# Mixers paced to slot 97, one route moved to the next phase, an eleventh row buffer and a 4 KB descriptor ring

## The chip, the cores and the metric

One core of one Trainium2 chip runs the whole kernel in one launch. The metric is the device time of that launch in microseconds. The kernel before takes 1519.63 us (median of three runs, 1519.27 to 1521.75).

## What is computed

A decoder trunk of two layers over one sequence of 256 tokens with 1024 channels, in float32. The reference, cut to what matters:

```python
for l in range(DEPTH):                       # 2 layers
    proj = x @ w_in[l]                       # 1024 -> 2464 columns, split over four mixers
    mix = concat([short_conv, mla_attention, conformer_conv, swa_sink_attention])
    mix = rms_norm_per_head(mix) * gain
    h = layer_norm(ALPHA * x + mix @ w_out[l])
    x = layer_norm(ALPHA * h + peer_ffn(h))

def peer_ffn(h):                             # per chunk of 128 tokens
    q = (h @ w_q).reshape(c, 8, 2, 128)      # 8 heads, two halves
    sc = einsum('chpd,hpnd->chpn', q, sub_keys)
    # top 16 of 128 in each half, then top 16 of the 256 sums: 16 expert numbers per head
    gate = softmax(best_s)
    act = gelu(einsum('chkd,cd->chk', u_tab[idx], h))
    return einsum('chk,chkd->cd', gate * act, v_tab[idx])
```

Each token picks 8 heads x 16 experts = 128 experts out of 16384, and each expert is one row of u and one row of v (1024 floats each). The rows of 256 tokens x 128 experts x 2 layers are most of what the kernel reads.

## The kernel before

**Tiles and phases.** The 256 tokens are two tiles of 128 (t = 0, 1). For each layer l and tile t there is a *phase* of 128 *slots*; in slot k every token of the tile gets its k-th expert. The four phases run one after another: (0,0), (0,1), (1,0), (1,1), here called phases 0 to 3. Ahead of them lie the mixer of (0,0) and the route of its first head.

**A slot** (`peer`, line 738): GpSimd (POOL) issues an indirect DMA that gathers one row per token, u and v side by side, 128 partitions x 8 KB, into a buffer `row` (line 760). VectorE (DVE) multiplies the u half with h and sums it (the *product*, line 763). For the slot before, `post` then runs GELU and the gate on ScalarE (ACT, lines 745, 746), makes a diagonal of the result (line 748), and TensorE (PE) multiplies that diagonal with the v half into the two PSUM accumulators (line 750), which the profile shows as four passes of 128x512.

**Row buffers.** `row` comes from the pool `gp` with `ROWS` = 10 buffers. A gather can be issued when a buffer's last matmul is done. The tiles for `w_out` of the later mixers (line 579, tag `row`) and, at the start, the pieces of `w_in` of the first layer take buffers of the same pool.

**Other work beside the slots.** A phase's slots leave room on PE, DVE and ACT, and other tasks are woven in:
- `route(l, t, hd)` (line 661) computes one head's expert numbers and gates: 32 passes for the queries (line 680), 4 for the scores (line 685), then the two rounds of top 16 on DVE (lines 655 to 659). A head must be routed before the slots that use it. The weights of a head are 1152 KB. Tile 0 uses the heads in the order 0 to 7, tile 1 in the order 5, 6, 7, 0, 1, 2, 3, 4 (`HEADS`).
- `mix(l, t)` (line 289) is a mixer with its projections, attention and convolutions, the output projection (line 585) and a layer norm. It loads nine pieces of `w_in` and four of `w_out`. The mixer of tile 1 must end before any head of tile 1 is routed.
- `finish` is the layer norm that ends a phase; it runs in slots 0 to 3 of the next.

**Weight buffers.** `load_w` (line 162) uses a pool of three buffers for pieces of `w_in` and heads' weights, issued on SyncE's queue (SP). Heads 0, 1, 2 have buffers of their own (`HELD`). Heads 5, 6, 7 (`KEPT`) are the *joint* heads: their weights are loaded for tile 0 and kept in the three buffers until tile 1 has been routed with them, so they load once.

**The order of the work** is written out in `main_loop` (line 852): a list of tasks with a first slot, a last slot and a cost (`MIX` = 111, `ROUTE` = 10.9, `TAIL` = 6.6). `paced` (line 805) steps through the slots and advances each task in proportion, so a mixer given slots 0 to 80 is spread evenly over them. `keep_behind` lets the engines' order stray from this by six slots. Before, tile 0's phase has heads 2 to 6 in slots 0 to 80 beside the mixer of tile 1, and then four routes in 48 slots: joint heads 5, 6 and 7 of tile 1 and head 7 of tile 0, two of them at once between slots 80 and 97.

Of the kernel before, what the change touches and what calls it, by code (L numbers as in the profile page):

```python
# [33 lines left out]
QK = KC * 256 + 256  # L34
PPC = 8 + 6 + 62 + 2

ROWS = 10

HELD = (0, 1, 2)
KEPT = (5, 6, 7)  # L40
# [20 lines left out]
MIX, ROUTE, TAIL = 111.0, 10.9, 6.6  # L61
# [3 lines left out]
def kernel(ctx: ExitStack, tc: tile.TileContext, x, positions, w_in, w_att, bcast, perch, lnrows, lncols,  # L65
                      w_out, w_qk, uv, ident, mla_mask, swa_dist, iota, invf, out):
    nc = tc.nc
# [6 lines left out]
    sp = ctx.enter_context(tc.tile_pool(name="sp", bufs=2))  # L74
    gp = ctx.enter_context(tc.tile_pool(name="gp", bufs=ROWS))
    pm = ctx.enter_context(tc.tile_pool(name="pm", bufs=4, space=bass.MemoryType.PSUM))
# [661 lines left out]
    def peer(l, t, h, acc):  # L738

        n = NH * TOPK  # L740
        order = HEADS[t]
        prev = None

        def post(k, act, row, gate):
            S.activation(act, act, AF.Gelu)  # L745
            S.activation(act, act, AF.Copy, scale=gate[:, k % TOPK:k % TOPK + 1])  # L746
            dg = gp.tile([P, P], F32, tag="dg", name="dg", bufs=3)
            S.activation(dg, idn, AF.Copy, scale=act)  # L748
            for j in range(2):
                nc.tensor.matmul(acc[j], dg, row[:, DM + j * 512:DM + (j + 1) * 512],  # L750
                                 start=(k == 0), stop=(k == n - 1))

        for k in range(n):
            while (l, t, order[k // TOPK]) not in R:
                yield None
            ix8, ix, gate = R[l, t, order[k // TOPK]]
            if ix8 is not None and k % TOPK < 8:
                ix = ix8
            row = gp.tile([P, 2 * DM], F32, tag="row", name="row")
            nc.gpsimd.indirect_dma_start(out=row, out_offset=None, in_=uv,  # L760
                                         in_offset=bass.IndirectOffsetOnAxis(ap=ix[:, k % TOPK:k % TOPK + 1], axis=0))
            act = gp.tile([P, 1], F32, tag="act", name="act", bufs=3)
            V.scalar_tensor_tensor(row[:, :DM], row[:, :DM], 1.0, h, op0=ALU.mult, op1=ALU.mult, accum_out=act)  # L763
            if prev is not None:
                post(*prev)
            prev = (k, act, row, gate)
            yield 1
        post(*prev)

    def finish(l, t, h, acc):  # L770
        hp = mp.tile([P, DM], F32, tag="S", name="hp2")
        for j in range(2):
            sl = slice(j * 512, (j + 1) * 512)
            V.scalar_tensor_tensor(hp[:, sl], h[:, sl], ALPHA, acc[j], op0=ALU.mult, op1=ALU.add)
        yield 1.2
        xo = xp.tile([P, DM], F32, tag="x", name=f"x{t}_{l}")
        yield from layer_norm(xo, hp, 4 * l + 2, out[t * P:(t + 1) * P, :] if l == L - 1 else None)
        X[t] = xo
# [5 lines left out]
    def mix(l, t):  # L784
        if t == 0:
            Y[l] = layer_state(l)
        H[l, t] = yield from mixer(l, t, Y[l], X[t])
# [17 lines left out]
    def paced(gather, tasks):  # L805

        spent = [0.0] * len(tasks)
        live = [True] * len(tasks)

        def step(i):  # L810
            c = next(tasks[i][0], "end")
            if c == "end":
                live[i] = False
            elif c:
                spent[i] += c

        k = 0
        while True:
            n = len(log)
            with tc.high_priority():  # L820
                c = next(gather, "end")
            if c == "end":
                break
            if c is None:
                raise RuntimeError(f"slot {k} is not routed")
            keep_behind(n, chain, back, LATE)
            n = len(log)
            for i, (g, a, b, cost) in enumerate(tasks):
                while live[i] and spent[i] < cost * (k + 1 - a) / (b - a):
                    step(i)  # L830
                if k >= b:
                    while live[i]:
                        step(i)
            keep_behind(n, back, chain, EARLY)
            k += 1
        for i in range(len(tasks)):
            while live[i]:
                step(i)

    rope_tables()  # L840
    ahead = mix(0, 1)
# [7 lines left out]
    def routes(l, t, spans):  # L849
        return [(route(l, t, hd), a, b, ROUTE) for hd, (a, b) in spans.items()]  # L850

    def main_loop():
        tail = None
        for i, (l, t) in enumerate(todo):
            acc = [pa.tile([P, 512], F32, tag=f"acc{j}", name="acc") for j in range(2)]
            tasks = [(tail, 0, 3, TAIL)] if i else []
            if t == 0:
                tasks += routes(l, 0, {1: (0, 3)} if l == 0 else {})
                tasks += routes(l, 0, {2: (0, 17), 3: (17, 32), 4: (32, 48), 5: (48, 64), 6: (64, 80)})
                tasks += [(mix(1, 1) if l else ahead, 0 if l == 0 else 3, 80, MIX)]  # L860
                tasks += routes(l, 1, {5: (80, 94)}) + routes(l, 0, {7: (84, 97)}) + routes(l, 1, {6: (97, 112), 7: (112, 128)})
            else:
                tasks += routes(l, 1, {0: (3, 20), 1: (20, 38), 2: (38, 56), 3: (56, 74), 4: (74, 92)})
                if l == 0:
                    tasks += [(mix(1, 0), 3, 98, MIX)] + routes(1, 0, {0: (98, 112), 1: (112, 126)})
            paced(peer(l, t, H[l, t], acc), tasks)
            tail = finish(l, t, H[l, t], acc)
        for _ in tail:
            pass

    main_loop()


# [80 lines left out]
```

## Time and profile before

| what | value |
|---|---|
| median of three runs | 1519.63 us (1519.27 to 1521.75) |
| the profiled execution | 1520.93 us, span 1518.9 us |
| PE, DVE, ACT, POOL busy | 88%, 72%, 39%, 42% of the span |
| TensorE's mean granted clock | 0.984 |
| moved by DMA | 614.47 MB, mean 405 GB/s |
| chain that ended last | PE 41%, DMA 31%, DVE 17%, ACT 5% |

The span runs from the first to the last instruction of the program; the device time holds it and a little around it. The chain is followed back from the last instruction, at each step to what released it. A stretch in which the DMA engines are at their full rate is limited by bytes; one in which they move less has a consumer or an issue that is late.

### The profile page before, as it was taken

The page shows a single profiled execution, that of the slowest core. Times are in us where ns is not written, and L with a number is a line of the kernel's source. Part 1 is how long each engine was busy: PE and PEld are TensorE (multiplying, and loading weights), DVE is VectorE, ACT ScalarE, POOL GpSimd, SP SyncE. Part 2 cuts the span into 40 slices and gives each one's busy share as a digit, 9 for nine tenths or more (in the row PEclk, how much of TensorE's full clock was granted, in tenths as well). Part 3 has the DMA queues.
Part 4 walks back from the last instruction along what each step waited for, and adds up shares of the span by engine and source line. Part 5 has one row for each costly group of instructions (what it writes and reads, how often), then busy time and mean ns, then how long its engine had stood idle before and what let it go on. Part 6 is the DMA issues. An engine that isn't in the chain of part 4 may idle for free.

```text
span 1518.9 us, 17527 instructions
## 1 busy us (share of the span) xinstructions
PE 1336.2 (88%) x4852; PEld 714.6 (47%) x4852; DVE 1096.7 (72%) x3161; ACT 590.1 (39%) x2047; POOL 632.3 (42%) x539
## 2 busy tenths in 40 slices
PE   8999979988989997889998989889998888888876
PEld 8576534444436653444445555544544433333222
DVE  5778887588767668876877667876887766676545
ACT  4233443334433324443343333542344334333332
POOL 2034333444554343444454333224355454655551
PEclk9999999999999999999999999899999999999999
DMA  9489999999999999999999999989999999999995
GB/s 383 177 324 426 426 428 396 385 401 424 426 426 427 426 426 427 420 389 426 427 427 426 427 426 427 411 334 407 419 426 428 426 427 426 427 427 427 427 427 220
DMA packets 86208, 614.47 MB, mean 405 GB/s; under 512 B 10336, under 2 KB 10720, under 8 KB 12768
## 3 DMA queue, kind: packets, MB, share of 16 engines
q0 software_dynamic: 73728, 536.90, 84.7%
q1 hardware_dynamic: 12096, 76.44, 12.3%
q8 instruction: 40, 0.66, 0.2%
q14 instruction: 56, 0.46, 0.1%
q10 hardware_dynamic: 288, 0.01, 0.0%
HBM read 612.26 MB, written 1.05 MB: 404 GB/s over the span
## 4 chain that ended last, share of the span: by engine, by line
PE 41%; DMA 31%; DVE 17%; ACT 5%; issue 4%; POOL 0%; DVEq 0%; POOLq 0%; SPq 0%; ACTq 0%
DMA row<-in_uv_dram,ix 31%; PE acc L750 24%; DVE row L763 7%; PE ps_q L680 6%; PE ps_o L585 3%; DVE cv L509 2%; ACT dg L748 1%; PE ps_cfa L319 1%; PE ps_mla L323 1%; ACT act L746 1%; PE ps_rs L685 1%; PE ps_scb L319 1%; ACT act L745 1%; PE po L284 1%; ACT L265 1%
## 5 line engine op out<-in xcount | busy, mean ns | idle before, releaser
L750 PE MATMUL acc<-row,dg 128*128 128x512 f32 x2048 | 977.9, 612 | 152.2 <-ACT dg L748 147.1
L760 POOL DMA_INDIRECT row<-in_uv_dram,ix x512 | 621.1, 1213 | 830.0 <-PE acc L750 272.5
L763 DVE SCALAR_TENSOR_TENSOR row<-row,h 128x1024 f32<-128x1024 f32 x512 | 619.2, 1219 | 217.2 <-DMA row<-in_uv_dram,ix 177.3
L750 PEld LDWEIGHTS acc<-row,dg 128*128 128x128 f32 x2048 | 364.1, 192 | 638.2 <-ACT dg L748 325.0
L745 ACT ACTIVATE act<-act 128x1 f32<-128x1 f32 x512 | 103.5, 202 | 586.2 <-DVE row L763 582.5
L748 ACT ACTIVATE dg<-idn,act 128x128 f32<-128x128 f32 x512 | 205.6, 402 | 24.8 <-PE acc L750 9.6
L746 ACT ACTIVATE act<-act,gate 128x1 f32<-128x1 f32 x512 | 150.2, 294 | 16.2 <-DVE gate L732 1.1
L680 PEld LDWEIGHTS ps_q<-hT,w_q_t 128*128 128x128 f32 x1024 | 124.1, 192 | 28.9 <-issue 27.3
L680 PE MATMUL ps_q<-hT,w_q_t 128*128 128x128 f32 x1024 | 126.9, 275 | 3.9 <-DVE hp L156 3.5
L509 DVE SCALAR_TENSOR_TENSOR cv<-cfu,pc,cv 128x128 f32<-128x128 f32 x217 | 67.6, 359 | 0.9
L585 PE MATMUL ps_o<-w_out_t,mT 128*128 128x512 f32 x128 | 60.9, 618 | 1.7 <-DVE mT L373 1.7
L655 DVE MAX8 tv<-rsc 128x8 f32<-128x128 f32 x64 | 18.5, 290 | 53.1 <-ACT rsc L687 47.5
L687 ACT COPY rsc<-ps_rs 128x128 f32<-128x128 f32 x64 | 17.0, 265 | 94.4 <-PE ps_rs L685 89.5
L683 ACT COPY rq<-ps_q 128x128 f32<-128x128 f32 x64 | 16.6, 259 | 66.2 <-PE ps_q L680 66.1
L763 DVE DVE_READ_ACCUMULATOR row<-row,h 128x1 f32 x512 | 42.2, 82 | 0.0
L585 PEld LDWEIGHTS ps_o<-w_out_t,mT 128*128 128x128 f32 x128 | 24.7, 198 | 31.0 <-issue 28.2
L685 PEld LDWEIGHTS ps_rs<-w_q_t,rq 128*128 128x128 f32 x128 | 22.9, 190 | 25.5 <-issue 20.9
L685 PE MATMUL ps_rs<-w_q_t,rq 128*128 128x128 f32 x128 | 24.7, 277 | 2.8 <-DVE hp L156 1.7
L323 PE MATMUL ps_mla<-w_in_t,xT 128*128 128x208 f32 x128 | 25.8, 353 | 0.6 <-ACT xT L118 0.5
L323 PEld LDWEIGHTS ps_mla<-w_in_t,xT 128*128 128x128 f32 x128 | 23.5, 199 | 3.9 <-issue 2.2
L649 DVE TENSOR_TENSOR grid<-tf,ab 128x512 f32<-128x512 f32 (+1 forms) x33 | 22.3, 674 | 0.6
L650 DVE TENSOR_REDUCE ex<-grid 128x32 f32<-128x512 f32 (+1 forms) x33 | 22.1, 671 | 0.6
(215 smaller groups left out, 958.7 us busy)
## 6 DMA issues: line engine op xcount, KB each, us to landing
w_in_t<-in_w_in_dram SPq DMA_DIRECT2D x24, 1024.0 KB, 9.5
w_q_t<-in_w_qk_dram SPq DMA_DIRECT2D x20, 1152.0 KB, 9.1
w_out_t<-in_w_out_dram SPq DMA_DIRECT2D x16, 1024.0 KB, 6.2
row<-in_uv_dram,ix POOLq DMA_INDIRECT x512
w_in_t<-in_w_in_dram SPq DMA_DIRECT2D x6, 832.0 KB, 8.7
att<-in_w_att_dram SPq DMA_DIRECT2D x2, 640.0 KB, 13.1
x<-in_x_dram SPq DMA_DIRECT2D x2, 512.0 KB
gb<-in_lnrows_dram SPq DMA_DIRECT2D x1, 1024.0 KB
```

What stands on the lines that cost most here:

```text
L319: nc.tensor.matmul(ps, w[:, c, j * P:(j + 1) * P], xT[:, c, :], start=(c == 0), stop=(c == KC - 1))
L323: nc.tensor.matmul(ps, xT[:, c, :], w[:, c, a:b], start=(c == 0), stop=(c == KC - 1))
L509: V.scalar_tensor_tensor(cv[j], src, wt, cv[j], op0=ALU.mult, op1=ALU.add)
L585: nc.tensor.matmul(po[j], mixed_T()[:, 2 * g + c, :], wg[:, c, j * 512:(j + 1) * 512], start=(n == 0 and c == 0), stop=(n == 3 and c == 1))
L680: nc.tensor.matmul(ps, wq[:, c, j * P:(j + 1) * P], hT[:, c, :], start=(c == 0), stop=(c == KC - 1))
L685: nc.tensor.matmul(ps, qT, w[:, KC * 256 + j * P:KC * 256 + (j + 1) * P], start=True, stop=True)
L745: S.activation(act, act, AF.Gelu)
L746: S.activation(act, act, AF.Copy, scale=gate[:, k % TOPK:k % TOPK + 1])
L748: S.activation(dg, idn, AF.Copy, scale=act)
L750: nc.tensor.matmul(acc[j], dg, row[:, DM + j * 512:DM + (j + 1) * 512], start=(k == 0), stop=(k == n - 1))
L760: nc.gpsimd.indirect_dma_start(out=row, out_offset=None, in_=uv, in_offset=bass.IndirectOffsetOnAxis(ap=ix[:, k % TOPK:k % TOPK + 1], axis=0))
L763: V.scalar_tensor_tensor(row[:, :DM], row[:, :DM], 1.0, h, op0=ALU.mult, op1=ALU.mult, accum_out=act)
```

## The change

Three edits. `ROWS` goes from 10 to 11. The program is made with a descriptor ring for GpSimd's DMAs of 4096 bytes per partition, where before the default stood. In the task list of tile 0's phases, the mixer ends at slot 97 instead of 80; head 7 of tile 0 is routed in slots 80 to 96 (84 to 97 before); joint heads 5 and 6 of tile 1 move to slots 97 to 126; and joint head 7 of tile 1 leaves this phase for slots 0 to 14 of the next. In tile 1's phases the other heads are shifted to make room: six routes in slots 0 to 94, where five stood in slots 3 to 92. The mixer of tile 1's phase (layer 0 only) stays at slots 3 to 98.

```diff
-ROWS = 10
+ROWS = 11
...
             if t == 0:
                 tasks += routes(l, 0, {1: (0, 3)} if l == 0 else {})
-                tasks += routes(l, 0, {2: (0, 17), 3: (17, 32), 4: (32, 48), 5: (48, 64), 6: (64, 80)})
-                tasks += [(mix(1, 1) if l else ahead, 0 if l == 0 else 3, 80, MIX)]
-                tasks += routes(l, 1, {5: (80, 94)}) + routes(l, 0, {7: (84, 97)}) + routes(l, 1, {6: (97, 112), 7: (112, 128)})
+                tasks += routes(l, 0, {2: (0, 17), 3: (17, 32), 4: (32, 48), 5: (48, 64), 6: (64, 80), 7: (80, 96)})
+                tasks += [(mix(1, 1) if l else ahead, 0 if l == 0 else 3, 97, MIX)]
+                tasks += routes(l, 1, {5: (97, 111), 6: (111, 126)})
             else:
-                tasks += routes(l, 1, {0: (3, 20), 1: (20, 38), 2: (38, 56), 3: (56, 74), 4: (74, 92)})
+                tasks += routes(l, 1, {7: (0, 14), 0: (14, 30), 1: (30, 46), 2: (46, 62), 3: (62, 78), 4: (78, 94)})
                 if l == 0:
                     tasks += [(mix(1, 0), 3, 98, MIX)] + routes(1, 0, {0: (98, 112), 1: (112, 126)})
...
-    nc = _bacc.Bacc("TRN2", target_bir_lowering=False, num_devices=1)
+    nc = _bacc.Bacc("TRN2", target_bir_lowering=False, num_devices=1, dynamic_dma_scratch_size=4096)
```

## Rows read from the trace of the kernel before

**Rows 1.** The page: busy us by engine, and the queue of the gathers.
```profile
PE 1336.2 (88%) x4852; PEld 714.6 (47%) x4852; DVE 1096.7 (72%) x3161; ACT 590.1 (39%) x2047; POOL 632.3 (42%) x539
...
q0 software_dynamic: 73728, 536.90, 84.7%
```

**Rows 2.** Busy time by stretch, late in phase 3, with the columns' names.
```profile
core 0: us, PE busy (x) PEld busy (x) DVE busy (x) ACT busy (x) POOL busy (x), PEclk, DMA share, GB/s
1210.00:1487.00 277.00, 233.02 (x607) 96.03 (x605) 174.01 (x387) 106.83 (x376) 154.67 (x112) 1.00 1.01 427
```

**Rows 3.** Busy time by stretch: the four phases, first to last product.
```profile
94.00:451.40 357.40, 320.87 (x1179) 173.15 (x1178) 279.81 (x849) 145.23 (x519) 152.32 (x132) 0.99 1.00 416
452.50:815.50 363.00, 326.64 (x1183) 176.40 (x1184) 265.53 (x747) 142.35 (x493) 155.72 (x128) 0.98 1.01 422
816.80:1186.90 370.10, 331.68 (x1248) 182.92 (x1248) 277.96 (x824) 147.30 (x513) 142.97 (x128) 0.99 1.00 413
1188.10:1506.10 318.00, 267.72 (x707) 111.65 (x708) 205.01 (x460) 121.65 (x426) 163.31 (x120) 1.00 0.99 418
```

**Rows 4.** Busy time by stretch: parts of phases 0, 1, 2, and the start.
```profile
94.00:331.60 237.60, 213.71 (x833) 120.28 (x833) 190.11 (x602) 96.66 (x339) 92.42 (x82) 0.99 1.00 413
452.50:717.50 265.00, 237.29 (x890) 131.96 (x891) 192.94 (x574) 104.05 (x356) 106.25 (x88) 0.97 1.01 420
816.80:1070.60 253.80, 226.53 (x907) 130.89 (x907) 188.92 (x579) 98.62 (x334) 84.97 (x79) 0.98 0.99 407
331.60:373.30 41.70, 36.63 (x137) 19.79 (x136) 33.87 (x107) 16.78 (x66) 18.11 (x16) 1.00 1.00 414
1070.60:1110.60 40.00, 34.93 (x133) 19.02 (x132) 33.87 (x107) 16.77 (x66) 17.23 (x15) 1.00 1.01 419
...
88.40:105.40 17.00, 15.87 (x127) 14.47 (x126) 14.50 (x65) 6.16 (x22) 8.83 (x9) 1.00 0.90 363
```

**Rows 5.** Line 763 in the first three of these stretches: how many products.
```profile
L763 DVE SCALAR_TENSOR_TENSOR row<-row,h x80: 1196/1218/1226, 94.0 to 330.4; 128x1024 f32<-128x1024 f32 x80
...
L763 DVE SCALAR_TENSOR_TENSOR row<-row,h x88: 1205/1218/1273, 452.5 to 715.1; 128x1024 f32<-128x1024 f32 x88
...
L763 DVE SCALAR_TENSOR_TENSOR row<-row,h x80: 1194/1218/1249, 816.8 to 1069.5; 128x1024 f32<-128x1024 f32 x80
```

**Rows 6.** The waits: us in total, times, longest.
```profile
POOL row L760 <- PE acc L750: 272.5, 166, 7.3
```

**Rows 7.** Busy time by stretch, in phase 2 around slot 50.
```profile
943.00:975.00 32.00, 23.37 (x81) 12.36 (x81) 23.42 (x84) 17.51 (x50) 7.54 (x8) 0.84 1.01 425
975.00:1007.00 32.00, 27.90 (x114) 15.64 (x113) 29.82 (x117) 16.89 (x51) 8.50 (x8) 1.00 0.86 325
1007.00:1033.00 26.00, 24.04 (x82) 12.59 (x82) 13.65 (x34) 7.79 (x32) 8.17 (x9) 1.00 0.97 377
```

**Rows 8.** The chain in order of time: start us, us, what, and how many passes.
```profile
1012.07 3.43 PE ps_o L585 x8
1015.50 1.78 PE ps_q L680 x16
1017.29 3.44 PE acc L750 x8
```

**Rows 9.** The page's groups: busy us, mean ns, then idle us before.
```profile
L760 POOL DMA_INDIRECT row<-in_uv_dram,ix x512 | 621.1, 1213 | 830.0 <-PE acc L750 272.5
L763 DVE SCALAR_TENSOR_TENSOR row<-row,h 128x1024 f32<-128x1024 f32 x512 | 619.2, 1219 | 217.2 <-DMA row<-in_uv_dram,ix 177.3
```

**Rows 10.** SP's queue in time order, 335 to 520 us: five issues from 343.6 on.
```profile
343.61 136.65 SPq L165 DMA_DIRECT2D w_in_t<-in_w_in_dram  x5
```

**Rows 11.** The page's DMA issues: size of one, and us from issue to landing.
```profile
w_in_t<-in_w_in_dram SPq DMA_DIRECT2D x24, 1024.0 KB, 9.5
```

**Rows 12.** POOL's and DVE's instructions in time order: the first gather and first product.
```profile
88.39 1.09 POOL L760 DMA_INDIRECT row<-in_uv_dram,ix  x1 [52.20 <-issue]
...
94.00 1.23 DVE L763 SCALAR_TENSOR_TENSOR row<-row,h 128x1024 f32<-128x1024 f32 x1 [0.79 <-DMA row<-in_uv_dram,ix]
```

## The prediction

> **What bounds the kernel now.** I read the page first, then busy time by stretch, then the chain and the waits. Most of the 1518.9 us span is the sixteen DMA engines at their limit: in a late stretch with only gathers and routes in it, 1210 to 1487 us, they move 427 GB/s with a DMA share of 1.01, while over the whole span PE, the busiest engine, stands at 88% and the software queue of the row gathers alone takes 84.7% of the sixteen engines' time [rows 1, 2]. So the time is bytes over 427 GB/s plus what the DMA stands below 427. No byte is added or taken away here, so only the second part can change.
>
> How large is it? Call the stretch from the first product on the gathered rows of one (layer, token tile) to the last a phase. The four ran at 416, 422, 413 and 418 GB/s [rows 3]. A stretch of length T at B GB/s has lost T x (427 - B)/427: 9.2, 4.3, 12.1 and 6.7 us. The last is the drain at the end of the program, which nothing here touches. The first three, **25.6 us**, are the prize. Nearly all of it lies in the part of each phase that carries a mixer: slots 0 to 80 of phase 0 (80 products of a row with h, 94 to 331.6 us) lose 237.6 x 14/427 = 7.8 us, slots 0 to 88 of phase 1 lose 265 x 7/427 = 4.3, slots 0 to 80 of phase 2 lose 253.8 x 20/427 = 11.9, together 24.0 [rows 4, 5]. The 17 slots after the mixer in phases 0 and 2, in which two routes run at once, ran at 414 and 419 GB/s and lose 1.3 and 0.7 [rows 4].
>
> Why the DMA falls short there: a gather is issued when one of the ten row buffers is free, and POOL's largest wait by far is for the last matmul on a row, 272.5 us in 166 waits [rows 6]. In a full stretch that is harmless, since the other rows are queued. In phase 2 it is not: from 943 to 975 us the DMA still ran at 425, living on its queue, while POOL found buffers for only 8 gathers in 32 us, where 13 would be the pace of 2.46 us; then the queue was empty, 325 GB/s for 32 us and 377 for the next 26, with DVE busy 29.8 of 32 us in the first and PE 24.0 of 26 in the second [rows 7]. Consumers were behind, not the DMA. PE's granted clock was 0.84 from 943 to 975, with PE busy only 23.4 of the 32 us, so part of that stretch ran at the lower of its two levels [rows 7].
>
> **The change part by part.** *Mixers over 97 slots instead of 80, in phases 0 and 2.* From the chain, 8 gather passes take 3.44 us, 16 query passes 1.78 and 8 output passes 3.43, so 0.43, 0.11 and 0.43 us each [rows 8]. A slot has 4 gather passes, 1.72 us. A route has 32 + 4 short passes, 4.0 us. Phase 1 has 1183 passes [rows 3]; less 512 for gathers and 7 x 36 for routes, a mixer (with the small tail of the layer before) has 419, of which 32 are output passes: 387 x 0.11 + 32 x 0.43 = 56 us of PE. Per slot of the mixer's stretch PE must work 1.72 + 4.0/16 + 56/80 = 2.67 us before and 1.72 + 0.25 + 56/97 = 2.55 after. The DMA's need comes from the bytes: 237.6 us x 413 GB/s = 98.1 MB over 80 slots, 2.87 us a slot at 427 in phase 0, and 103.3 MB, 3.02 us, in phase 2. Seventeen more slots bring 17.8 MB of rows and one head's weights, 1.2 MB, so 2.83 and 2.95. PE's share of the DMA's time falls from 93.0 to 90.1% and from 88.4 to 86.4%; the mean of the two from 90.7 to 88.3%. DVE is lower, 190.1 of 237.6 us, and falls with it [rows 4].
>
> *One route more in phase 1 and phase 3.* The same instructions, so nothing is added in sum; its 36 passes (4.0 us) leave slots 112 to 128 and enter slots 0 to 14 of the next phase. It issues no DMA, since its weights are kept; but on SP the loads behind it wait longer for that buffer (a rival below). Head 7 of tile 0 loads its weights four slots earlier, into a buffer that the mixer's pieces have left by then: nothing. Its DVE work is at most 10 us: phase 3 has 205.0 us of DVE, less 128 x 1.21 for the products, over five routes [rows 3, 9]. Phase 3 has no mixer and DVE idles a third of it: nothing. Phase 1, with five routes in 95 slots, stands at (1.72 + 5 x 4.0/95 + 56/95) = 2.52 us of PE against 265 x 420/88 = 1.265 MB a slot, 2.96 us: 85.1%; with six it is 2.56, 86.5%.
>
> Shares turn into lost time by the only two points I have: 85.1% lost 4.3 us, and 90.7% lost (7.8 + 11.9)/2 = 9.85, so 1.0 us per point. After: phases 0 and 2 at 88.3% lose 7.5 each, phase 1 at 86.5% loses 5.7. This line is the weakest step: phase 2 lost more than phase 0 at a lower share, because its work comes in lumps. Bounds of this part: no gain (lumps only move), and all of the 12 us by which phases 0 and 2 exceed phase 1.
>
> *Eleven row buffers.* No trace here has an eleventh. One more row is 1.05 MB, 2.46 us of queue, which a hole eats before the DMA idles. Bounds: nothing (the w_out tiles of the mixer use these buffers too), and 2.46 us for each of some seven separate holes, 17 us. I take it once for each of three phases, 7.4 us, as the holes of one phase follow each other without the queue filling in between [rows 7]. At the very start slots 0 to 7 run at 363 GB/s for 17 us, 2.5 us lost [rows 4]; what gates them is the first index as much as a buffer, so I take 0 and keep 2.5 for the lower end.
>
> *The two routes at once in slots 80 to 97* are gone, and their 2.0 us; those slots now belong to the 97-slot stretch costed above.
>
> *The 4 KB ring.* [...] Its price is not in the trace. POOL issues take 1.213 us on average and POOL is idle 830 us [rows 9], so a longer issue is hidden up to twice its length; the cover goes only if POOL must wait for the queue to empty, which is a rival. Taken: 0.
>
> **Sum:** 24.0 + 2.0 lost now; left after 7.5 + 7.5 + 5.7 - 7.4 = 13.3; gain 12.7, say 12.5. The profiled execution took 1520.9 us (span 1518.9), 1.3 above the median of 1519.6. So 1508.4 for such a profile and **1507 us** for the median; own range 1499 to 1514: with the eleventh buffer worth nothing, and with it worth twice what I took.
>
> [...] The rows have 427 GB/s for 277 us on end [rows 2]. [...]
>
> **The rivals.**
> *All of it comes back.* If each hole is just covered by the extra row and the thinner mixer, 25.6 us return, some 1494, and 2.5 less with the start. For it: holes of 2 to 3 us beside 2.46 us of buffer. Against: phase 2's hole of 7.6 us.
>
> *Phase 1 gives it back.* Head 7's weights now keep one of three weight buffers until slot 14 of phase 1. Now five weight loads for that mixer are issued from 343.6 us on, the first in phase 0 [rows 10]; then at most two can be early. Each piece takes some 9.5 us to land [rows 11]; if three come that late, PE stands 28.5 us, of which some 19 us of queued rows (ten buffers less two in the consumers' hands, 2.46 us each) hide all but 9.5. With the extra route's 4.0 us that is 13.5, and the time is some 1520. Against: in phase 1's first half the DMA, full with weights, is the slow side.
>
> *The ring waits (slower).* If POOL, each time the ring is used up, must let the queue drain, each drain costs the time from an empty queue to the first product, 94.0 - 88.4 = 5.6 us, less one row, so 3.2 us [rows 12]. [...] It decides from four drains on. [...]
> [...]
>
> **How the numbers follow.** About 0.2% (3 us) is what a measurement of this kernel tells from no change. Forecast 0.60 (faster), all back 0.13 (faster), phase 1 0.16 (of it 0.12 within 0.2%, 0.04 slower), ring 0.11 (slower). Faster 0.73, same 0.12, slower 0.15. The range must leave out at most 0.2: below, the all-back case to 1496; above, the phase 1 case as far as 1519. What is left out is the ring and the worse end of phase 1.
>
> **What would show it.** Right: phases 0 and 2 at 418 GB/s or more, phase 1 near 423, phase 3 unchanged, POOL's wait for the row matmuls no longer in one block near slot 50 of phase 2, and in a full stretch one row more between the issue of a gather and its product. The phase 1 rival shows as PE waiting on w_in_t loads and a phase 1 longer than 363 us. The ring shows as regular gaps of POOL of some 5 us in phase 3. The forecast is wrong if phase 2's 325 GB/s stretch stays, only later.

## The result and the profile after

The kernel after takes 1528.1 us (median of six runs, 1524.94 to 1530.08) against 1519.45 us for the kernel before beside it: ratio **1.0052**, 95% interval 1.0040 to 1.0064. It is 0.52% slower. The prediction, 1507.0 us within 1496 to 1519 and 73% for faster, was wrong in its sign. The profiled execution took 1530.08 us, its span 1528.0.

The page of the kernel after, busy us by engine and the gathers' queue:

```profile
PE 1337.5 (88%) x4852; PEld 716.2 (47%) x4852; DVE 1094.3 (72%) x3161; ACT 590.5 (39%) x2049; POOL 628.8 (41%) x539
...
q0 software_dynamic: 73728, 536.90, 84.4%
```

Against [rows 1] the work is the same: as many passes, as many packets, busy times within 4 us. (ACT's two further instructions are table loads, 22 where before has 20.) So the 9.2 us between the two profiled executions (1530.08 against 1520.93) are waiting. Busy time by stretch, kernel after: the four phases, then a stretch late in phase 3, then four pieces of phase 2 around slots 40 to 70:

```profile
core 0: us, PE busy (x) PEld busy (x) DVE busy (x) ACT busy (x) POOL busy (x), PEclk, DMA share, GB/s
93.80:448.40 354.60, 317.17 (x1160) 171.22 (x1160) 271.92 (x812) 145.80 (x511) 145.22 (x132) 0.99 1.00 416
449.70:819.50 369.80, 330.50 (x1205) 177.42 (x1204) 270.08 (x784) 143.59 (x501) 151.11 (x128) 0.99 1.00 418
820.70:1195.70 375.00, 331.12 (x1226) 181.53 (x1227) 272.02 (x787) 144.24 (x505) 148.01 (x128) 0.98 0.98 405
1196.90:1515.20 318.30, 268.60 (x730) 115.02 (x728) 211.85 (x497) 122.73 (x434) 166.34 (x120) 1.00 0.99 418
...
1215.00:1490.00 275.00, 233.56 (x642) 101.15 (x641) 181.30 (x424) 107.66 (x383) 153.79 (x110) 1.00 1.01 427
...
941.00:975.00 34.00, 25.84 (x108) 14.04 (x106) 29.62 (x105) 16.45 (x52) 12.71 (x10) 1.00 1.01 426
975.00:1010.00 35.00, 27.63 (x106) 15.94 (x107) 24.43 (x90) 11.89 (x36) 6.75 (x7) 0.90 0.85 327
1010.00:1033.00 23.00, 18.61 (x57) 9.46 (x56) 15.46 (x45) 12.54 (x40) 6.97 (x6) 0.85 0.80 277
1033.00:1057.00 24.00, 21.25 (x74) 10.70 (x73) 19.39 (x66) 8.72 (x30) 8.56 (x8) 1.00 0.98 386
```

By the prediction's own measure, T x (427 - B)/427, the first three phases lose 354.6 x 11/427 = 9.1, 369.8 x 9/427 = 7.8 and 375.0 x 22/427 = 19.3 us, together **36.3** (unrounded terms) where [rows 3] gave 25.6. Phase 3 is as long as before (318.3 and 318.0), and its middle again runs at 427 GB/s. Phase 2 lost most: the hole of [rows 7] (325, 377 GB/s) is there again, in much the same place (49 products of phase 2 start before 975 us in both kernels) but longer and deeper: 327 GB/s for 35 us, 277 for 23, 386 for 24. Over the 58 us from 975 to 1033 no engine is full: PE is busy 46.2 us, DVE 39.9, ACT 24.4. In one piece of it an engine is: from 987.8 to 1003.7 us DVE works 15.6 of 15.9 us, while PE works 9.2.

The waits of the kernel after in those 58 us: us in total, times, longest:

```profile
POOL row L760 <- PE acc L750: 27.6, 8, 7.8
...
ACT act L745 <- DVE row L763: 17.3, 9, 4.9
PE acc L750 <- ACT dg L748: 13.8, 8, 4.2
...
DVE mT L373 <- PE ps_mT L372: 7.5, 2, 4.6
```

Everyone waits for everyone: POOL for PE's row passes, PE for ACT's diagonal, ACT for DVE's product, and DVE for PE's transposes. The chain of the kernel after in time order, two pieces of the hole (start us, us, what; x2 of line 763 is one product with the reading of its sum):

```profile
994.96 1.14 DVE row L763 x2
996.10 0.34 DVE grid L633
996.43 0.08 DVE rs_u L102
996.51 0.33 DVE ct L521
...
998.83 0.47 DVE bj L659 x2
...
1000.22 0.17 DVE rs_y L111
1000.46 0.30 issue
1000.76 1.24 DVE row L763 x2
1002.02 0.21 ACT act L745
1002.25 0.30 ACT act L746
1002.58 0.41 ACT dg L748
1003.03 3.13 PE acc L750 x4
...
1014.34 0.20 ACT act L745
1014.56 1.28 ACT L265
1015.91 0.37 issue
1016.27 0.68 ACT S_mla L265 x3
1016.95 0.18 ACT act L746
1017.13 0.98 ACT S_mla L265 x4
1018.12 0.30 ACT dg L748
1018.46 3.78 PE acc L750 x4
```

The kernel writes one list of instructions for each engine, with the slots, the mixer and the routes in it, and a slot's row goes DVE, ACT, PE. From one product at 994.96 to the next at 1000.76 DVE works through a route's top 16 (`grid`, `bj`), a norm of the mixer's attention (`rs_u`, `rs_y`) and one of its convolution (`ct`): 5.8 us for a slot whose pace should be 2.46. PE stands 3.47 us, and its next four row passes take 3.13 us where [rows 8] give 1.72: the granted clock over just these passes, 1003.03 to 1006.16 us, is 0.61, so part of them ran at the lower of its two levels: it stands at 1.00 up to 1003.6 us, at 0.50 from 1004.0 to 1006.8 and at 1.00 again from 1007.6 to 1017.2 (in the kernel before, in the first stretch of [rows 7], at 0.50 from 949 to 955 us, 1.00 from 956 to 962, 0.50 from 963 to 965 and 1.00 from 966 to 975). At 1014.34 ACT has begun a slot's `post`, but before the diagonal stand a table load (line 265 at 1014.56) of 1.28 us and the softmax of an attention (`S_mla`), with the slot's gate (line 746) between its pieces: the diagonal comes at 1018.12, PE has stood 4.18 us, and four passes take 3.78 us, at a granted clock of 0.50 from 1018.46 to 1022.24 us, the lower level all through. The first activation after the table load starts 0.02 us after the load ends (ACT's instructions in time order, kernel after):

```profile
1014.56 1.28 ACT L265 ACT_TABLE_LOAD   x1
...
1015.86 0.51 ACT L265 ACTIVATE S_mla<-S_mla,nm 128x256 f32<-128x256 f32 x1
```

### The profile page after: what moved, and what is told of

Its sections match the earlier page's. It is cut to its first block, busy times and chain, and to the rows that moved or that the text cites. A ratio compares the mean times of both kernels' runs of the same rounds, so it can differ in the third digit from the quotient of the medians.

```text
span 1528.0 us, 17507 instructions
## 1 busy us (share of the span) xinstructions
PE 1337.5 (88%) x4852; PEld 716.2 (47%) x4852; DVE 1094.3 (72%) x3161; ACT 590.5 (39%) x2049; POOL 628.8 (41%) x539
## 4 chain that ended last, share of the span: by engine, by line
PE 42%; DMA 27%; DVE 22%; ACT 6%; issue 3%; POOL 0%; DVEq 0%; SPq 0%; POOLq 0%; ACTq 0%
DMA row<-in_uv_dram,ix 26%; PE acc L750 25%; DVE row L763 9%; PE ps_q L680 5%; PE ps_o L585 4%; DVE cv L509 2%; ACT dg L748 1%; PE ps_mla L323 1%; ACT act L746 1%; PE ps_sch L319 1%; PE ps_cfa L319 1%; PE ps_scc L319 1%; PE ps_rs L685 1%; ACT act L745 1%; PE ps_swq L319 1%
## 5 line engine op out<-in xcount | busy, mean ns | idle before, releaser
L748 ACT ACTIVATE dg<-idn,act 128x128 f32<-128x128 f32 x512 | 205.6, 402 | 26.4 <-PE acc L750 11.6
L680 PEld LDWEIGHTS ps_q<-hT,w_q_t 128*128 128x128 f32 x1024 | 122.8, 192 | 21.0 <-issue 20.3
L683 ACT COPY rq<-ps_q 128x128 f32<-128x128 f32 x64 | 16.6, 259 | 73.9 <-PE ps_q L680 73.9
L685 PEld LDWEIGHTS ps_rs<-w_q_t,rq 128*128 128x128 f32 x128 | 22.7, 190 | 31.3 <-issue 26.1
L685 PE MATMUL ps_rs<-w_q_t,rq 128*128 128x128 f32 x128 | 25.5, 281 | 7.7 <-DVE hp L156 5.9
L649 DVE TENSOR_TENSOR grid<-tf,ab 128x512 f32<-128x512 f32 (+1 forms) x33 | 22.3, 675 | 0.7
## 6 DMA issues: line engine op xcount, KB each, us to landing
row<-in_uv_dram,ix POOLq DMA_INDIRECT x512, 18.7
att<-in_w_att_dram SPq DMA_DIRECT2D x2, 640.0 KB, 10.2
```

Of the source, the lines that this page charges most:

```text
L680: nc.tensor.matmul(ps, wq[:, c, j * P:(j + 1) * P], hT[:, c, :], start=(c == 0), stop=(c == KC - 1))
L685: nc.tensor.matmul(ps, qT, w[:, KC * 256 + j * P:KC * 256 + (j + 1) * P], start=True, stop=True)
```

## The experiments

The theories. **R**: the ring costs. **S**: the weights of heads 5, 6, 7, loaded early, take DMA time inside the mixer's stretch. **M**: the mixer that ends late costs by itself, since its chains of short dependent steps then stand in the engines' queues between the slots. **L**: the loss is a draw, set by the order in which the scheduler happens to write the queues, which every edit reshuffles. For all kernels, the loss by the same measure (first to last product of each phase, B as the windows give it); a row landing on the other side of a boundary shifts some 2.5 us between neighbours, so the sum is firmer than its parts. It is no exact price either: against the kernel before, sum and span of a trace part by up to 5 us, either way (e9_after_mix80 has 7.9 us less loss and a span shorter by 3.6; e10_after_mix88 5.3 and 10.6).

| kernel | mixer end, buffers | lost in phases 0, 1, 2 | sum | ratio to before (95%) |
|---|---|---|---|---|
| before | 80, 10 | 9.2, 4.3, 12.1 | 25.6 | 1 |
| after | 97, 11 | 9.1, 7.8, 19.3 | 36.3 | 1.0052 (1.0040 to 1.0064) |
| e2_ring4k | 80, 10 | 6.6, 4.3, 13.9 | 24.8 | 1.0009 (0.9995 to 1.0022) |
| e1_rows11 | 80, 11 | 10.9, 6.0, 0.8 | 17.7 | 0.9966 (0.9953 to 0.9980) |
| e8_move_mix80 | 80, 11 | 11.7, 5.2, 0.8 | 17.7 | 0.9965 (0.9953 to 0.9978) |
| e9_after_mix80 | 80, 11 | 12.6, 3.4, 1.7 | 17.7 | 0.9970 (0.9953 to 0.9987) |
| e6_rows11_fetch | 80, 11 | 15.3, 6.8, 3.4 | 25.5 | 0.9977 (0.9962 to 0.9992) |
| e11_after_mix72 | 72, 11 | 2.5, 8.6, 8.6 | 19.6 | 0.9963 (0.9950 to 0.9976) |
| e10_after_mix88 | 88, 11 | 7.4, 5.2, 7.7 | 20.3 | 0.9936 (0.9917 to 0.9955) |
| e7_after_mix95 | 95, 11 | 8.3, 6.9, 14.8 | 30.0 | 0.9994 (0.9978 to 1.0009) |
| e3_sched_rows10 | 97, 10 | 7.4, 0.0, 23.9 | 31.3 | 1.0030 (1.0017 to 1.0042) |
| e4_mix97_no_move | 97, 11 | 8.3, 6.9, 16.6 | 31.9 | 1.0020 (1.0008 to 1.0033) |
| e5_after_fetch | 97, 11 | 13.4, 6.0, 15.7 | 35.2 | 1.0044 (1.0030 to 1.0057) |
| e17_after_w88 | 97, 11 | 13.4, 6.9, 13.1 | 33.4 | 1.0054 (1.0032 to 1.0075) |
| e18_after_w77 | 97, 11 | 10.8, 9.6, 12.1 | 32.5 | 1.0038 (1.0026 to 1.0051) |
| e15_before_defer2 | 80, 10, deferred | 14.4, 0.8, 10.2 | 25.5 | 0.9978 (0.9968 to 0.9987) |
| e16_rows11_defer2 | 80, 11, deferred | 4.1, 2.6, 15.6 | 22.3 | 0.9955 (0.9938 to 0.9972) |
| e13_defer2_mix80 | 80, 11, deferred | 3.3, 2.6, 13.8 | 19.7 | 0.9956 (0.9939 to 0.9973) |
| e14_defer2_mix88 | 88, 11, deferred | 4.1, 0.9, 9.4 | 14.3 | **0.9933** (0.9915 to 0.9951) |
| e12_after_defer2 | 97, 11, deferred | 4.1, 1.7, 12.9 | 18.7 | 0.9941 (0.9923 to 0.9960) |

**The change taken apart.** Buffers and ring alone, ring alone, and the new list alone:

```diff
 e1_rows11, against before: ROWS = 11, dynamic_dma_scratch_size=4096
 e2_ring4k, against before: dynamic_dma_scratch_size=4096
 e3_sched_rows10, against after: ROWS = 10, no dynamic_dma_scratch_size
```

> The kernel before with 11 row buffers and the 4 KB ring, task list untouched. Theory S (the new task list costs: the mixer's work was moved into slots whose DMA need is only rows, 2.46 us each, because the heads' weights are fetched long before): the buffer itself helps, 2.5 us per hole, 1510 to 1517 us. Theory R (the ring or the buffer costs): 1525 us or more, phase 3 longer than 318 us. Theory L (any edit shuffles the engines' queues and moves the time by some us): anywhere from 1514 to 1525, with phases that move without a pattern.

> The kernel before with the 4 KB ring alone; every engine's queue of instructions is the same as before. S and L: 1519 to 1521 us, no change. R by the ring: 1525 us or more, with POOL's issues longer than 1.21 us on average or regular gaps in phase 3.

> The changed task list with 10 row buffers and the default ring. S: the list alone costs more than the whole change, since the eleventh buffer is missing: 1530 to 1537 us. R: the list is not the cause, 1507 to 1515 us. L: 1518 to 1533.

Measured: 1515.64 against 1520.45 us; 1521.35; 1525.10. R falls: the ring alone leaves the time where it was. The slowdown comes with the list; with the old list the eleventh buffer comes with a gain. For e3_sched_rows10 both S and R forecast wrongly, and only L's wide band holds. Busy time by stretch of e1_rows11, phases 0 to 2:

```profile
93.70:452.20 358.50, 324.56 (x1185) 175.95 (x1184) 278.35 (x849) 144.23 (x517) 152.04 (x132) 0.98 1.00 414
453.80:817.70 363.90, 324.10 (x1183) 176.16 (x1182) 264.76 (x747) 141.87 (x493) 154.73 (x128) 0.97 1.01 420
819.10:1181.30 362.20, 330.81 (x1249) 183.65 (x1247) 276.90 (x824) 145.50 (x513) 153.22 (x128) 0.98 1.01 426
```

The gain is all in phase 2 (426 GB/s for 413); phases 0 and 1 gained nothing. For a buffer that is odd. Compared instruction by instruction (share that lies in matching runs, worst of DVE, PE and ACT, from slot 30 to the mixer's end), the queues of e1_rows11 match those of before to 0.92 in phase 0 and 0.95 in phase 1, but to only 0.67 in phase 2, so the edit of the buffer was an edit of the order too, as theory L has it. Where two kernels have one order in phase 2 (1.00), they lose alike: before and e2_ring4k 12.1 and 13.9, e1_rows11 and e8_move_mix80 0.8 and 0.8, after and e4_mix97_no_move 19.3 and 16.6. In the new list (e3_sched_rows10 to after) the eleventh buffer gained nothing: the sum grew from 31.3 to 36.3.

**The moved head and the early weights.**

```diff
 e4_mix97_no_move, against after
-                tasks += routes(l, 1, {5: (97, 111), 6: (111, 126)})
+                tasks += routes(l, 1, {5: (97, 107), 6: (107, 117), 7: (117, 128)})
 (tile 1's list as in the kernel before)
 e8_move_mix80, against before: ROWS = 11, ring 4096, and
-... + routes(l, 1, {6: (97, 112), 7: (112, 128)})
+... + routes(l, 1, {6: (97, 112)})
 (tile 1's list as in the kernel after)
 e5_after_fetch against after, e6_rows11_fetch against e1_rows11
+FETCH = ((5, 42), (6, 58), (7, 74))
...
+    def fetch(l, hd):
+        w = wp.tile([P, KC * 288], F32, tag="w", name="w_q_t")
+        V.memset(w[:, 0:1], 0.0)
+        held[l, hd] = load_w(w_qk, (l * NH + hd) * P * QK, QK, "w_q_t", w)
+        yield 1
...
+                tasks += [(fetch(l, hd), s, s + 1, 1) for hd, s in FETCH]
```

> The changed kernel with head 7 of tile 1 routed in phases 0 and 2 again (slots 117 to 128) and tile 1's phases as before; mixers to slot 97, 11 buffers, 4 KB ring. S: phase 1 goes back from 371 to 362 to 365 us, phase 2 stays at 375 or more: 1519 to 1523 us in all. A theory that the moved head is the whole cause: 1507 to 1513 us, phase 2 below 368. R: 1525 or more.

> The kernel before with 11 buffers and the 4 KB ring and only the last joint head moved into the next phase; mixers end at slot 80 as before. Theory S: phase 2 as in the 11-buffer kernel (363 us), phase 1 longer by some 5 us (370): 1517 to 1522 us. If the moved head were free: 1512 to 1516. Theory L: phase 2 back above 368 though nothing in it was touched but the end.

> The changed kernel, but the weights of heads 5, 6, 7 in tile 0's phases are fetched no earlier than some six slots before slots 42, 58 and 74 (a one-column write on DVE that the load waits for) instead of all three as soon as buffers are free, near slot 40. Theory S (weights fetched early leave the mixer's last slots with rows alone, and starve the rows before them): phase 2 loses under 10 us of DMA time where the changed kernel loses 19, and the time is 1512 to 1521. Theory L (the order of the engines' queues decides, not where the bytes lie): phase 2 anywhere from 365 to 380 us, the loss not moved in one direction.

> The kernel before with 11 buffers, the 4 KB ring and the same late fetches. Theory S: phase 0 loses less than the 13.9 us of the 11-buffer kernel without them, 1504 to 1512 us. Theory L: 1510 to 1522, phase 2 may be worse than without.

Measured: 1524.70 (against 1520.45), then 1517.56, 1529.26 and 1518.66 us (against 1522.56). With the mixer at 80 the moved head is nearly free: the sum stays at 17.7 (e1_rows11 to e8_move_mix80), and phase 1 grows by 2.7 us (363.9 to 366.6) while phase 0 shrinks by 1.1. With the mixer at 97 (e4_mix97_no_move to after) it is not: phase 1 grows by 3.0 (366.8 to 369.8), the sum by 4.4 and the ratio from 1.0020 to 1.0052, with intervals that do not overlap. S falls: fetching late by a write of DVE into one column, which the load must wait for, moved two of phase 2's three loads from 944.9 and 954.2 us to 996.9 and 1048.9 and gained nothing, and phase 0 lost 4 us more. (The 13.9 us in the expectation of e6_rows11_fetch stands as 10.9 in the table, and the 12.1, 4.8 and 12.8 of e15_before_defer2 below as 9.2, 4.3 and 12.1.)

**The mixer's end alone.** One number of the kernel after is changed, 97 to 95, 88, 80 or 72:

```diff
-                tasks += [(mix(1, 1) if l else ahead, 0 if l == 0 else 3, 97, MIX)]
+                tasks += [(mix(1, 1) if l else ahead, 0 if l == 0 else 3, 80, MIX)]
```

> The changed kernel with the mixer's end at slot 95 instead of 97, nothing else. Theory S: 1526 to 1529 us, the phases within 2 us of the changed kernel's. Theory L: some phase moves by 4 us or more, in either direction.

> The changed kernel with the mixer of tile 0's phases ending at slot 80 instead of 97, nothing else. Theory M (the later end itself costs: the mixer's dense part, softmax, group norms and output projection, meets slots 54 to 88, where rows come at full rate, and each of its lumps stalls the chain product, diagonal, matmul): phase 2 back to 363 to 367 us, 1514 to 1520 in all. Theory L (each order of the queues is a draw): phase 2 anywhere from 363 to 378.

> The same with the end at slot 88. Theory M: between the two, phase 2 from 366 to 372 us, its lost time between those of ends 80 and 95. Theory L: no order between 80, 88, 95 and 97.

> The same with the end at slot 72: the mixer is denser. Theory M: phase 2 no worse than with 80 as long as the dense part stays ahead of slot 50, 362 to 366 us. The forecast's reading (what counts is PE's work per slot): worse than with 80, since PE's work per slot rises from 2.67 to 2.75 us. Theory L: no order.

Measured: 1520.82 (against 1522.56), then 1517.28, 1512.56 and 1515.83 us (against 1521.90). From 97 back to 80 the loss halves, 36.3 to 17.7; the three phases together get 13.4 us shorter (first product of phase 0 to first product of phase 3). The sum is level up to 88 (19.6, 17.7, 20.3 for 72, 80, 88), then 30.0 and 36.3 for 95 and 97. M's bands hold for the ends 80 and 88 (phase 2, first product to that of phase 3, 363.8 and 366.1 us); with 72 it takes 367.1, 1 us above the band. With 95, S's band is missed, and no phase became 4 us longer or shorter, as L had it. The forecast's reading, a denser mixer being worse, does not show: 72 and 80 are not told apart in time. Part of what e7_after_mix95 and e10_after_mix88 gain lies ahead of the phases: their first product comes at 90.1 and 90.2 us, not 93.8. Busy time by stretch of e9_after_mix80, phases 0 to 2:

```profile
94.50:452.60 358.10, 320.52 (x1160) 173.79 (x1159) 272.43 (x812) 143.83 (x510) 152.97 (x132) 0.98 1.00 412
453.80:819.20 365.40, 325.74 (x1205) 175.73 (x1204) 269.16 (x784) 143.51 (x501) 147.85 (x128) 1.00 1.01 423
820.50:1183.00 362.50, 327.87 (x1226) 182.60 (x1226) 271.32 (x787) 144.54 (x505) 155.53 (x128) 0.98 1.01 425
```

The counts of passes and instructions of phase 2 are those of the kernel after (1226 and 787), the GB/s 425 for 405.

**The slot's chain given a slot of slack.** `post` is done two products later instead of one, so that ACT and PE have another slot's time to answer DVE; the arithmetic is the same. In the kernel after, at ends 80 and 88, in the kernel before, and in e1_rows11:

```diff
 e12_after_defer2
-            act = gp.tile([P, 1], F32, tag="act", name="act", bufs=3)
+            act = gp.tile([P, 1], F32, tag="act", name="act", bufs=4)
...
-            if prev is not None:
-                post(*prev)
-            prev = (k, act, row, gate)
+            if len(prev) == 2:
+                post(*prev.pop(0))
+            prev.append((k, act, row, gate))
...
 e13_defer2_mix80, e14_defer2_mix88: the same, mixer end 80, 88
 e15_before_defer2: the same in before; e16_rows11_defer2: the same in e1_rows11
```

> The changed kernel with the second half of a slot (GELU, gate, diagonal, matmul) issued two slots after the product instead of one, so that a lump on DVE or ACT does not leave PE without a diagonal; one row buffer more is held by it. Theory M, in that the chain's latency makes the hole: phase 2 loses under 12 us where the changed kernel loses 19, PE's waits for the diagonal in slots 40 to 80 of phase 2 fall well below 20 us, 1515 to 1524 us. If the hole is sheer work (throughput): no better, 1526 to 1532, since a buffer is lost.

> The changed kernel with the deferral by two slots and the mixer's end at 80. If the chain's latency is all that makes a late mixer dear: phase 2 within 2 us of the deferred kernel with end 97 (368), 1509 to 1516 us. If the place of the dense part counts by itself: phase 2 at 360 to 364, some 5 us below it, 1504 to 1512.

> The same with the end at 88, the best end without deferral. Latency alone: phase 2 at 366 to 369, 1509 to 1515 us. Place too: phase 2 at 361 to 366, 1503 to 1510.

> The kernel before (10 buffers, default ring, its own task list) with the deferral by two slots alone. Latency theory: its 12.1, 4.8 and 12.8 us of lost DMA time shrink though one buffer more is held, 1508 to 1516 us. If deferral works only with the eleventh buffer: 1518 to 1526.

> The kernel before with 11 buffers, the 4 KB ring and the deferral, its own task list. Latency theory: below the kernel before with deferral by the buffer's worth, 1503 to 1511 us. Place theory: phase 2 at 363 us or less, as with 11 buffers without deferral.

Measured: 1513.76 (against 1521.90), then 1514.45, 1510.44, 1516.57 and 1513.90 us (against 1520.20). With the late end the slack halves the loss, 36.3 to 18.7, and the ratio goes from 1.0052 to 0.9941. With the end at 80 it gains nothing in the sum (17.7 to 19.7 and 22.3 with eleven buffers, 25.6 to 25.5 with ten), though their times are 0.1 to 0.2% lower. With the end at 88 the sum falls from 20.3 to 14.3, but the time stays (0.9936 and 0.9933), as the first product of e10_after_mix88 came 3.6 us sooner. So what the late end costs is what slack for a slot's chain gives back: its latency. One late order was tried with slack. Not all bands held: e12_after_defer2 beat M's time though its phase 2 lost 12.9 us, not under 12; e15_before_defer2 and e16_rows11_defer2 came in 0.6 and 2.9 us above the latency bands, so for the early end latency is not borne out. The place theory's bands for e13_defer2_mix80 and e16_rows11_defer2 were missed; e14_defer2_mix88 does not decide. Waits of PE in slots 40 to 80 of phase 2, of the kernels before, after, e9_after_mix80 and e12_after_defer2 in turn:

```profile
PE acc L750 <- ACT dg L748: 13.6, 8, 5.4
```

```profile
PE acc L750 <- ACT dg L748: 20.4, 14, 4.2
```

```profile
PE acc L750 <- ACT dg L748: 11.6, 5, 5.4
```

```profile
PE acc L750 <- ACT dg L748: 12.2, 10, 3.7
```

PE waits for the diagonal 20.4 us in the kernel after, and 11.6 to 13.6 in the others. The same wait, read over the same slots in all twenty traces, is 16.6 to 20.4 us in the seven undeferred kernels with the end at 95 or 97 and 6.5 to 13.6 in the other thirteen. It marks the late end; it does not follow the loss of phase 2 from kernel to kernel (13.6 with 12.1 lost before, 11.6 with 1.7 in e9_after_mix80).

**The order alone.** M and L were still mixed, since every new end also brought a new order. These two keep the kernel after, each instruction and its list, and change only by how many slots the engines' orders may stray (the order in phase 2 then matches that of after to some 0.7):

```diff
-EARLY, LATE = 6, 6
+EARLY, LATE = 8, 8     (e17_after_w88; 7, 7 in e18_after_w77)
```

> The kernel after with the scheduler's slack between the engines' queues set to eight slots instead of six, nothing else: same task list, buffers, ring, same instructions, but another order of them in the three engines' queues. Theory L (the loss of phase 2 follows the order that the scheduler happens to write): phase 2 is a new draw, anywhere between 363 and 378 us (the kernel after has 376.2), and the time between 1513 and 1530. Theory M (the mixer that ends at slot 97 costs by itself, whatever the order): phase 2 stays between 373 and 379 us and the time between 1524 and 1531.

> The same with a slack of seven slots: a third order of the same instructions. Theory L: again a draw of its own, phase 2 between 363 and 378 us, and of the two kernels of this pair at least one differs from the kernel after by 4 us or more in phase 2. Theory M: phase 2 between 373 and 379 us here as in its pair, time 1524 to 1531.

Measured: 1529.89 and 1526.29 us, against 1520.22. Phase 2, from its first product to that of phase 3, takes 374.1 and 371.7 us (the kernel after 376.2). Busy time by stretch, phases 0 to 2, of e17_after_w88 and then e18_after_w77:

```profile
93.20:451.90 358.70, 321.05 (x1163) 172.10 (x1162) 271.26 (x812) 145.47 (x511) 145.16 (x132) 0.98 1.00 411
453.10:821.40 368.30, 330.36 (x1204) 178.86 (x1205) 269.70 (x784) 144.30 (x501) 146.35 (x128) 0.98 1.00 419
822.70:1195.50 372.80, 329.19 (x1228) 180.20 (x1228) 272.50 (x787) 143.95 (x503) 148.42 (x128) 1.00 0.99 412
```

```profile
92.40:447.60 355.20, 317.43 (x1163) 172.73 (x1162) 271.29 (x812) 142.89 (x509) 145.38 (x132) 0.99 1.00 414
448.80:820.40 371.60, 329.50 (x1205) 177.93 (x1205) 269.77 (x784) 144.14 (x501) 149.01 (x128) 0.99 1.00 416
821.60:1192.10 370.50, 331.46 (x1228) 181.22 (x1229) 271.91 (x787) 143.30 (x503) 145.85 (x128) 0.99 1.00 413
```

Each theory has a part. The order moves the loss between the phases: phase 2 from 19.3 to 13.1 and 12.1, phase 0 from 9.1 to 13.4 and 10.8. M's band for phase 2 (373 to 379 us) is missed by one of the two. But the sum stays at 33.4 and 32.5, and both times lie in M's band. All seven undeferred kernels with the end at 95 or 97 lose 30.0 to 36.3 us; the undeferred ones that end at 72, 80 or 88 with eleven buffers lose 17.7 to 20.3, or 25.5 with the late fetch. By plain length, first product of phase 0 to first product of phase 3, those seven take 1098.0 to 1103.5 us and the eight undeferred ones that end by 88, with ten buffers or eleven, 1087.6 to 1095.1. These are not fifteen independent orders: e1_rows11, e8_move_mix80 and e9_after_mix80 share theirs in phases 0 and 2 (matching to 0.97 and more), as after and e4_mix97_no_move do, so three equal sums of 17.7 are close to one draw. **M holds for the sum, L for where it falls.** The number of table loads is not the cause: e18_after_w77 has 18 and loses 32.5 us. What stays open is why the cost appears between 88 and 95: which of the mixer's chains meets which route there was not tried by itself.

## Why the prediction was wrong

*What bounds the kernel: right.* The middle of phase 3 ran at 427 GB/s again, and the time moved with the lost DMA time: 36.3 - 25.6 = 10.7 us of loss, 9.2 of time. The forecast left 13.3 us of loss; 36.3 came.

*Mixers over 97 slots: the step that failed.* It turned PE's share per slot into lost time, 1.0 us per point, and so let 24.0 us fall to 20.7. The mixer's end alone (e9_after_mix80 to after) brings +18.6 us of loss instead, 13.4 in the length of the three phases. An average share says how much work a slot has; the loss comes from how long a slot's row takes through DVE, ACT and PE when each has a mixer's and a route's steps queued ahead. Spreading the mixer left the work as it was and left those chains without slack: over the hole as a whole no engine is full, and one slot of slack took 17.6 us of the loss back (36.3 to 18.7). The prediction had called this line its weakest step, as work comes in lumps, yet bounded the part below by "no gain". It needed a bound for a loss.

*The eleventh buffer, 7.4 us: failed in the list that it was forecast for, and right in size with the old one by luck.* From e2_ring4k to e1_rows11 the sum falls 24.8 to 17.7, so 7.1 us. But the step had 2.46 us in each of three phases; phase 2 gave 13.1, and phases 0 and 1 lost 4.3 and 1.7 more. With the end at 97 (e3_sched_rows10 to after) the sum grew by 5.0. Taken in this order, the list alone cost 5.7 us (25.6 to 31.3) where the forecast had a gain of 5.3, and the buffer 5.0 where it had a gain of 7.4: the two terms fail by about as much. How much a buffer covers depends on the order it finds; what made it cost something here was not traced.

*Two routes at once, 2.0 us: not told apart* from the mixer's stretch, which now covers those slots. *The ring, 0: right*, and with it the slower rival fell: no run shows how many gathers a ring of either size serves, but e2_ring4k shows 427 GB/s over the stretch of [rows 2]. *The start, 0: right*: from 88.4 to 105.4 us the DMA ran at 362 GB/s, [rows 4] 363.

*The moved head: nearly right for phase 1, and short for the whole.* Phase 3 is unchanged. Phase 1 was given 1.4 us more (4.3 to 5.7) and got longer by 2.7 to 3.0, though its own loss moved by -0.8 and +0.9. With the late end the sum over three phases grew by 4.4 us with that head, most of it in phase 2. The first half of the rival on phase 1 came true: weight loads of that mixer are issued from 386.1 us on, where [rows 10] had 343.6 (SyncE's queue of the kernel after, in time order):

```profile
386.08 119.80 SPq L165 DMA_DIRECT2D w_in_t<-in_w_in_dram  x7
```

Its second half did not: in the first 190 us of phase 1 PE's waits name no load, and the longest is 2.8 us.

*What would show it.* Of the sign given for wrong, the 325 GB/s stretch staying, only later, the first half came: 327 GB/s from 975 us, hardly later, and 277 after it. Of the signs for right only phase 3 came: phases 0, 1 and 2 ran at 416, 418 and 405 GB/s.

## What to carry to other kernels

Where work of several tasks is woven into one queue per engine, an engine's average share does not tell what a thinner spread brings. Read in the hole itself which wait follows which, and count how long one item takes through all its engines; if no engine is full over it, try slack for that chain (here one slot more between product and `post`: with the mixer's end at 97 the ratio went from 1.0052 to 0.9941, with it at 80 or 88 the gain is 0.0014 and 0.0003, inside the intervals, and in the kernel before 0.0022). And before a gain is put down to a buffer or a list, run the same kernel in another order: here one phase moved by 6 to 7 us from the order alone, while the sum over phases moved by 3 to 4.

## What the runs showed of the hardware that was not expected

A table load stands as 1.28 us in ACT's queue with nothing after it, yet together with the softmax behind it the load held one slot's diagonal from 1014.56 to 1018.12 us and PE for 4.2 us. Four row passes after such stops, of 3.47 and 4.18 us, took 3.13 and 3.78 us, at granted clocks of 0.61 and 0.50 over the passes themselves, where after stops of 1.65 and 1.02 us (at 991.19 and 994.63 us) they took 1.98 at 1.00: these two stops of PE cost again after they had ended. A descriptor ring of 4 KB in place of the default one cost nothing that can be measured (1.0009, 0.9995 to 1.0022).
